# Gathering expert tokens by pairs of units, with one-hots as the stationary operand

## The chip, the cores and the metric

The kernel runs on one core of a Trainium2 chip. The metric is the time of one execution on the device in microseconds (us), as a median of several runs. Before the change the median of three runs was 1506.28 us (1504.05 to 1506.33).

## The reference

Two layers of one trunk. In each, a mixer (Fourier mixing, differential attention, a gated linear recurrence) is followed by a mixture of experts. Layer 0 computes 256 context and 256 latent tokens, layer 1 in the mixture only the latent ones. The part that matters here is the mixture; the reference sorts the token slots by expert, and for each block of one expert e does:

```python
D_MODEL = 1024; D_EXPERT = 512; N_EXPERTS = 32; TOP_K = 2
# wts: weight of a token's two experts; toks, ws: tokens and weights of a block's slots
xb = xpad[toks]
hb = jax.nn.silu(xb @ w1[e]) * (xb @ w3[e])
yb = (hb @ w2[e]) * ws[:, None]
acc = acc.at[toks].add(yb)
```

All weights are float32. One expert has six tiles of 1 MB, so the experts of both layers are 384 tiles, most of what the kernel reads.

## The kernel before

**Tiles.** S() gives a large tile of 128 x 2048 floats (1 MB) out of N_S = 22, W() a small one of 128 x 512 out of N_W = 11, PS() one of eight PSUM banks. Large tiles hold weights as they stream in, but also residuals, rows of modulation and split tokens. In the expert stage of layer 0, seven large tiles are taken otherwise: one of residuals, one of gating rows, four of tokens (hh and hl, the tokens' high and low parts) and the gathered tokens xt; a second xt lives for a while when the next group is gathered. In layer 1 it is four.

**The weight stream.** All weights form one list of tiles in the order of use. issue() (L169) writes their DMAs into the program of the SyncE (SP), which carries them out in order; a DMA waits until the tile that had its large tile before is released by its last reader. ahead(FIRST[l]) (L1711) asks for the first tiles of an expert stage, more() (L1612) for as many new ones as have been used up, ROOM[l] tiles ahead.

**Units.** The experts are ordered by how many tokens they have. units_of() (L31) makes units of 64 token slots: a unit serves one expert with 64 slots or two with 32 each. Two units are a pair (p), two pairs a group (g). Per pair moe() (L1365) does for each of two units: the ups (up, L1450: 64 slots times w1 and w3), act (L1461), transposing the hidden values (hid_t, L1466), and the downs (down, L1474: times w2). combine() (L1489) adds the pair before to the residuals while the ups of the next pair run. onehot_t() (L1436) makes the transposed one-hots for it.

**Before the first unit.** Routing ends with rmx (L1302), each token's place in each slot range. Then, in the order of the program: onehot(0) (L1385, one-hots of a group), order() (L1312, the experts' order, which the SyncE needs for addresses), late() (L1323, the routing weights, in three bfloat16 parts wb, and at its end the counts of an overflow), gather(0) (L1397), and the units. gather(g) has the tokens as the stationary operand and the one-hots moving, so that the result comes out transposed, as the ups want it; slot_weights() (L1417) casts the one-hots and multiplies them with wb. gather(g + 1) comes at the end of a group's second pair. No scheduler moves anything: each engine does its instructions in the order in which the program writes them, and waits for others by semaphores. PE is the TensorE, DVE the VectorE, ACT the ScalarE, POOL the GpSimd.

Of the kernel before, what the change touches and what calls it, by code (L numbers as in the profile page):

```python
# [50 lines left out]
NCOL = [3 * len(u) for u in UNITS]  # L51
N_S = 22
N_W = 11

# [15 lines left out]
def tile_backbone(  # L70
# [991 lines left out]
    def proj_prep(l, mixh, mixl, raw, pre, ends):  # L1062
# [242 lines left out]
        nw = nc_ // 6 * 4  # L1305
        wb = tiny([128, nt, nw, 3], "wb", 1, BF)
        wv = tiny([128, 2, nt], "wv", 1)
# [15 lines left out]
        def late():  # L1323
# [19 lines left out]

            for i in range(3):
                V.tensor_copy(wb[:, :, :, i], wx[0])
                if i < 2:
                    V.tensor_tensor(out=wx[0], in0=wx[0], in1=wb[:, :, :, i], op=OP.subtract)

# [12 lines left out]

        r.update(rmx=rmx, wb=wb, wv=wv, ec=ec, cap=cap, rem=rem, nbi=nbi, order=order, late=late)
        return r

    def moe(l, r):  # L1365
# [9 lines left out]

        def hsl(t, i, d):
            a = (i % 2) * D + d * 128
            return t[i // 2][:, a:a + 128]

        ohs, xts, wss, ots = {}, {}, {}, {}  # L1380

        def pairs_in(g):
            return min(2, np_ - 2 * g)

        def onehot(g):  # L1385

            o = tp.tile([128, 4, 2, 3, 64], FR, name="oh", tag="oh", bufs=1)
            n = pairs_in(g) * 6
            for i in range(nt):
                V.tensor_tensor(  # L1390
                    out=o[:, i].rearrange("p a b (h s) -> p (a b h) s", h=2)[:, 0:n],
                    in0=iota[:, None, :].to_broadcast([128, n, 32]),
                    in1=r["rmx"][:, i, 12 * g:12 * g + n][:, :, None].to_broadcast([128, n, 32]),
                    op=OP.is_equal)
            ohs[g] = o

        def gather(g):  # L1397

            o = ohs[g]
            m = pairs_in(g)  # L1400
            xt = S()
            for dd in range(4):
                ps = PS()
                for j in range(2):
                    d = 2 * dd + j
                    n = 0
                    for i in range(nt):
                        for t in (hh, hl):
                            mm(ps[:, j * 256:j * 256 + m * 128], hsl(t, i, d),
                               o[:, i, 0:m, 0:2].rearrange("p a b s -> p a (b s)"), n == 0, n == 2 * nt - 1)  # L1410
                            n += 1
                (V.tensor_copy if dd % 2 else A.copy)(v3(xt[:, dd * 512:(dd + 1) * 512], 256)[:, :, 0:m * 128],  # L1412
                                                      v3(ps, 256)[:, :, 0:m * 128])
            xts[g] = xt
            slot_weights(g)

        def slot_weights(g):  # L1417
            o = ohs[g]
            m = pairs_in(g)
            ob = wp.tile([128, 4, 256], BF, name="w", tag="w")  # L1420
            for i in range(nt):
                A.copy(ob[:, i, 0:m * 128].rearrange("p (a s) -> p a s", a=m),
                       f(o[:, i, 0:m, 0:2].rearrange("p a b s -> p a (b s)")))
            pw = PS()
            for pr in range(m):
                for i in range(nt):
                    mm(pw[:, pr * 16:pr * 16 + 12], ob[:, i, pr * 128:(pr + 1) * 128],
                       r["wb"][:, i, 4 * (2 * g + pr):4 * (2 * g + pr + 1), :].rearrange("p a b -> p (a b)"),
                       i == 0, i == nt - 1)
            ws = tiny([128, 2], "ws", 2)  # L1430
            for q in range(4):
                rr = slice(32 * q, 32 * q + 32)
                V.reduce_sum(ws[rr, 0:m], pw[rr, 0:16 * m].rearrange("p (a b) -> p a b", b=16)[:, :, 3 * q:3 * q + 3], axis=AX.X)
            wss[g] = ws

        def onehot_t(p):  # L1436

            o = ohs[p // 2]
            res = []
            for q in range(2):  # L1440
                pt = PS()
                for i in range(nt):
                    src = o[:, i, p % 2].rearrange("p b s -> p (b s)")[:, 64 * q:64 * q + 128]
# [181 lines left out]

        onehot(0)
        r["order"]()
        state["lim"] = first_1 + LIM if l == 0 else 1 << 30
        r["late"]()
        gather(0)  # L1630
        prev = None
        taken = {}
        for p in range(np_):
            sh = W()
            for q in range(2):
                u = 2 * p + q
                g = u // 4
# [5 lines left out]
                xt = xts[g]  # L1643
                m = u % 4
                end = u + 1 == len(units) and l in LAST
                if end:
                    px, py = PS(), PS()
                    down(ht, wd, px[0:64, :], py[64:128, :])
                ph = PS()
                for ks in UPS[q]:  # L1650
                    up(u, lambda k: xt[:, k * 256 + m * 64:k * 256 + (m + 1) * 64], ws, ph, ks)
# [3 lines left out]
                act(u, ph, wss[g][a:a + 64, m // 2:m // 2 + 1], sh)  # L1655
                if not again:
                    more(4 * len(ranks))
                if q == 0:
                    onehot_t(p)
                    if m == 2 and 4 * (g + 1) < len(units):  # L1660
                        onehot(g + 1)
                elif end:
                    spin(SPE[l], hh[0])
                else:
                    px, py = PS(), PS()
                    down(ht, wd, px[0:64, :], py[64:128, :])
                if q and units[u - 1][0] != ranks:
                    more(2 * len(wd))
                ht, wd = hid_t(u, sh, PS()), ws
            if p % 2 == 1 and u + 1 < len(units):  # L1670
                gather(g + 1)
            down(ht, wd, px[64:128, :], py[0:64, :])
# [127 lines left out]
```

## Time and profile before

| | |
|---|---|
| median of three runs | 1506.28 us |
| the profiled execution | 1505.11 us, of which 1503.3 us span from first to last instruction |
| busy: TensorE, VectorE, ScalarE, GpSimd | 1295.8, 623.1, 372.7, 364.8 us |
| moved by DMA | 489.66 MB, 326 GB/s over the span |
| expert stage of layer 0 | from about 339 us (routing done) to about 825 us |
| expert stage of layer 1 | from about 1037 us to the end |

The time of an engine that is busy tells little here: a stage has its own limit. The page's slices of the span show the DMA engines full in two long stretches and mostly not in the mixers, which lie before 310 and between 829 and 1030 us.

### The profile page before, as it was taken

Reading aid. Unit: us, or ns where it says so; the run is one execution under the profiler, and the core shown is the slowest. Engines: PE = TensorE matmul, PEld = TensorE weight load, DVE = VectorE, ACT = ScalarE, POOL = GpSimd, SP = SyncE. Lnnn points to the kernel's source line nnn. Section 1 sums busy time; section 2 is a strip of 40 time slices with the busy share of each in tenths; the row PEclk is TensorE's granted clock in tenths of the full one; section 3 lists DMA queues with packets and bytes.
Section 4 is the critical chain, followed back from the end, with each engine's and each line's share of the span. In section 5 each row is a group of like instructions: output and inputs, shape, how many; then the busy total and the mean of one; then the engine's idle time right before and its main releaser. Section 6 shows DMA issues by size and latency. Waiting matters only on the chain. (4 is left out here: it accounts for less than half of the span.)

```text
span 1503.3 us, 18776 instructions
## 1 busy us (share of the span) xinstructions
PE 1295.8 (86%) x6910; PEld 683.5 (45%) x6910; DVE 623.1 (41%) x1209; ACT 372.7 (25%) x763; POOL 364.8 (24%) x402
## 2 busy tenths in 40 slices
PE   5989998978999898989897999787989779787775
PEld 3767544765545353535352876365334223232231
DVE  3587587663333323232224678876212112111111
ACT  3333675321111110101012544842111001010010
POOL 2333012530243322222222551051111111101110
PEclk9999999988999999999999999898999999989898
DMA  9943352275999999999999924084999999999995
GB/s 346 388 151 120 119 207 93 85 305 204 421 421 405 421 420 421 420 421 421 420 421 386 383 91 136 34 312 186 420 420 420 421 421 420 421 421 421 421 421 244
DMA packets 101498, 489.66 MB, mean 326 GB/s; under 512 B 10411, under 2 KB 13081, under 8 KB 52249
## 3 DMA queue, kind: packets, MB, share of 16 engines
q1 hardware_dynamic: 96752, 485.11, 80.1%
q10 hardware_dynamic: 4649, 3.29, 0.8%
q8 instruction: 56, 0.92, 0.2%
q14 instruction: 41, 0.34, 0.1%
HBM read 487.32 MB, written 1.05 MB: 325 GB/s over the span
## 5 line engine op out<-in xcount | busy, mean ns | idle before, releaser
L125 PE MATMUL ps<-s 128*32 128x512 f32 (+3 forms) x2488 | 527.8, 611 | 85.0 <-DMA s<-in_w 81.1
L125 PEld LDWEIGHTS ps<-s 128*32 128x32 f32 (+2 forms) x2488 | 172.5, 138 | 398.3 <-issue 220.7
L1500 POOL TENSOR_TENSOR xres<-xres,w 128x512 f32<-128x512 f32 x92 | 116.7, 1295 | 420.6 <-DVE w L1499 420.6
L1464 DVE SCALAR_TENSOR_TENSOR w<-w,ws,ps 64x512 f32<-64x512 f32 x48 | 35.9, 747 | 402.2 <-ACT w L1463 402.2
L125 PE MATMUL ps<-s,ht 128*32 128x512 f32 (+1 forms) x1056 | 177.8, 596 | 8.0 <-ACT ht L1471 7.2
L125 PE MATMUL ps<-w,s 128*128 128x512 f32 x672 | 167.7, 402 | 1.3 <-POOL w L526 0.6
L1463 ACT ACTIVATE w<-ps 64x512 f32<-64x512 f32 x48 | 28.4, 592 | 553.5 <-PE ps L125 553.5
L1500 POOL TENSOR_TENSOR s<-s,w 128x512 f32<-128x512 f32 x50 | 63.2, 1287 | 364.6 <-DVE w L1499 364.6
L125 PEld LDWEIGHTS ps<-w,s 128*128 128x128 f32 x672 | 126.7, 192 | 33.5 <-issue 4.4
L526 POOL TENSOR_TENSOR w<-s,w 128x512 fp32r<-128x512 f32 x80 | 109.9, 1384 | 119.5 <-ACT w L525 101.1
L1499 DVE TENSOR_TENSOR w<-ps,s 128x512 f32<-128x512 f32 x148 | 91.1, 683 | 66.1 <-PE ps L125 66.1
L125 PE MATMUL ps<-s,w 128*128 128x512 f32 (+2 forms) x480 | 104.7, 369 | 5.2 <-DVE s L519 2.4
L125 PEld LDWEIGHTS ps<-s,ht 128*32 128x32 f32 (+1 forms) x1056 | 50.6, 122 | 111.4 <-issue 98.3
L125 PEld LDWEIGHTS ps<-s,w 128*128 128x128 f32 x480 | 78.0, 203 | 36.1 <-issue 13.9
L125 PE MATMUL ps<-w 128*128 128x512 f32 (+1 forms) x392 | 89.9, 381 | 2.4 <-ACT w L1485 1.4
L1486 DVE TENSOR_TENSOR w<-ps,w 128x512 fp32r<-128x512 f32 x48 | 30.9, 686 | 135.0 <-ACT w L1485 135.0
L125 PE MATMUL ps<-oh,s 128*128 128x256 f32 (+1 forms) x640 | 83.6, 293 | 0.0
L125 PEld LDWEIGHTS ps<-w 128*128 128x128 f32 x392 | 67.4, 198 | 34.6 <-issue 18.0
L125 PEld LDWEIGHTS ps<-oh,s 128*128 128x128 f32 x640 | 81.1, 202 | 3.2 <-issue 2.4
L1412 DVE COPY s<-ps 128x512 f32<-128x512 f32 (+1 forms) x26 | 16.8, 649 | 92.9 <-PE ps L125 86.2
L125 PE MATMUL ps<-s,cond 128*32 128x512 f32 x336 | 54.9, 637 | 0.0
L525 ACT CAST w<-s 128x512 fp32r<-128x512 f32 x80 | 48.3, 620 | 4.3 <-issue 1.4
(260 smaller groups left out, 1145.1 us busy)
## 6 DMA issues: line engine op xcount, KB each, us to landing
s<-in_w SPq DMA_DIRECT2D x384, 1024.0 KB, 19.8
s<-in_w_mod SPq DMA_DIRECT2D x48, 1024.0 KB, 12.5
s<-in_w_in SPq DMA_DIRECT2D x18, 1024.0 KB, 14.5
s<-in_w_out SPq DMA_DIRECT2D x8, 512.0 KB, 6.2
s<-in_w_out SPq DMA_DIRECT2D x4, 1024.0 KB, 8.7
s<-in_const_b SPq DMA_DIRECT2D x2, 768.0 KB, 15.4
s<-in_xc SPq DMA_DIRECT2D x2, 512.0 KB, 4.5
xres<-in_x SPq DMA_DIRECT2D x2, 512.0 KB, 7.5
```

The source lines that it names most:

```text
L125: PE.matmul(o, l, r, start=start, stop=stop)
L525: A.copy(wh[:, 0:n], src)
L526: G.tensor_sub(wl[:, 0:n], src, f(wh[:, 0:n]))
L1412: (V.tensor_copy if dd % 2 else A.copy)(v3(xt[:, dd * 512:(dd + 1) * 512], 256)[:, :, 0:m * 128], v3(ps, 256)[:, :, 0:m * 128])
L1463: A.activation(sh[a:a + 64, :], ps[a:a + 64, :], AF.Silu)
L1464: V.scalar_tensor_tensor(sh[a:a + 64, :], sh[a:a + 64, :], ws, ps[64 - a:128 - a, :], op0=OP.mult, op1=OP.mult)
L1486: V.tensor_sub(yl, ps, f(yh))
L1499: V.tensor_tensor(out=t, in0=ps, in1=g2[:, gg:gg + 512], op=OP.mult)
L1500: (V if end and h else G).tensor_add(xr_(tt, c), xr_(tt, c), t)
```

## The change

Tokens are gathered for one pair at a time. The one-hots are now the stationary operand and 512 columns of token rows move; the result has a slot per partition, is copied into two small tiles (rows), transposed (turn) and copied into two small tiles more (xts). The slot weights are multiplied with the one-hots as they are, wb has two float32r parts. A large tile less (N_S = 21), three small ones more (N_W = 14), and ROOM and FIRST of layer 0 are 15 instead of 14.

The order changes: gather(0) stands ahead of order(), turn(0) between order() and late(), the slot weights behind late(); the last part of late() becomes left(), called after the first unit. Later, gather(p + 1) stands ahead of the first downs of pair p, turn(p + 1) and slot_weights(p + 1) ahead of the second.

```diff
-N_S = 22
-N_W = 11
+N_S = 21
+N_W = 14
-        wb = tiny([128, nt, nw, 3], "wb", 1, BF)
+        wb = tiny([128, nt, nw, 2], "wb", 1, FR)
-            for i in range(3):
-                V.tensor_copy(wb[:, :, :, i], wx[0])
-                if i < 2:
-                    V.tensor_tensor(out=wx[0], in0=wx[0], in1=wb[:, :, :, i], op=OP.subtract)
+            V.tensor_copy(wb[:, :, :, 0], wx[0])
+            V.tensor_tensor(out=wb[:, :, :, 1], in0=wx[0], in1=f(wb[:, :, :, 0]), op=OP.subtract)
+
+        def left():
...
-        def onehot(g):
-            o = tp.tile([128, 4, 2, 3, 64], FR, name="oh", tag="oh", bufs=1)
+        def onehot(p):
+            o = tp.tile([128, 4, 3, 64], FR, name="oh", tag="oh", bufs=2)
...
-                            mm(ps[:, j * 256:j * 256 + m * 128], hsl(t, i, d),
-                               o[:, i, 0:m, 0:2].rearrange("p a b s -> p a (b s)"), n == 0, n == 2 * nt - 1)
+        def slots(p, i):
+            return ohs[p][:, i, 0:2].rearrange("p b s -> p (b s)")
+        def gather(p):
+            rows[p] = []
+            for h in range(2):
+                ps = PS()
+                n = 0
+                for i in range(nt):
+                    for t in (hh, hl):
+                        c = i % 2 * D + h * 512
+                        mm(ps, slots(p, i), t[i // 2][:, c:c + 512], n == 0, n == 2 * nt - 1)
+                        n += 1
+                t = W()
+                (V.tensor_copy if h else A.copy)(t, ps)
+                rows[p].append(t)
+        def turn(p):
+            xts[p] = []
+            for t in rows.pop(p):
+                ps = PS()
+                for k in range(4):
+                    PE.transpose(ps[:, k * 128:(k + 1) * 128], t[:, k * 128:(k + 1) * 128], ident)
+                x = W()
+                (V.tensor_copy if xts[p] else A.copy)(x, ps)
+                xts[p].append(x)
+        def slot_weights(p):
+            pw = PS()
             for i in range(nt):
-                A.copy(ob[:, i, 0:m * 128].rearrange("p (a s) -> p a s", a=m),
-                       f(o[:, i, 0:m, 0:2].rearrange("p a b s -> p a (b s)")))
+                mm(pw[:, 0:8], slots(p, i), r["wb"][:, i, 4 * p:4 * p + 4, :].rearrange("p a b -> p (a b)"),
+                   i == 0, i == nt - 1)
...
         onehot(0)
+        gather(0)
         r["order"]()
         state["lim"] = first_1 + LIM if l == 0 else 1 << 30
+        turn(0)
         r["late"]()
-        gather(0)
+        slot_weights(0)
...
-                    if m == 2 and 4 * (g + 1) < len(units):
-                        onehot(g + 1)
+                    if p + 1 < np_:
+                        onehot(p + 1)
+                    if p == 0:
+                        r["left"]()
...
                 else:
+                    if p + 1 < np_:
+                        gather(p + 1)
                     px, py = PS(), PS()
                     down(ht, wd, px[0:64, :], py[64:128, :])
...
-            if p % 2 == 1 and u + 1 < len(units):
-                gather(g + 1)
+            if p + 1 < np_:
+                turn(p + 1)
+                slot_weights(p + 1)
             down(ht, wd, px[64:128, :], py[0:64, :])
...
-    ROOM = 14, 17
-    FIRST = 14, 17
+    ROOM = 15, 17
+    FIRST = 15, 17
```

**Where instructions move.** First, the TensorE at the start of layer 0's expert stage, before. The row with utri is the last of routing, `ps<-w,ones 128x32` is order()'s matmul, `ps<-oh,s` the gather, `ps<-wb,w` the first of eight slot-weight matmuls, behind which stand the ups (`ps<-s 64x512`).

```order
L125 MATMUL ps<-w,utri 128x78
L125 LDWEIGHTS ones
L125 MATMUL ps<-w,ones 128x32
L125 MATMUL ps<-oh,s 128x256 x64
L125 LDWEIGHTS w
L125 MATMUL ps<-wb,w 128x12
```

And the same place now, to the first downs (`ps<-s,ht`). L1415 are the transposes of turn(), L1439 those of onehot_t(), L1464 those of hid_t().

```order
L125 MATMUL ps<-w,utri 128x78
L125 MATMUL ps<-s,oh 128x512 x16
L125 LDWEIGHTS ones
L125 MATMUL ps<-w,ones 128x32
L1415 MATMUL ps<-ca,w 128x128 x8
L125 MATMUL ps<-wb,oh 128x8 x4
L125 MATMUL ps<-s,w 64x512 x16
L1439 MATMUL ps<-ca,oh 128x128 x8
L1464 MATMUL ps<-ca,w 128x64 x4
L125 MATMUL ps<-s,w 64x512 x16
L125 MATMUL ps<-s,oh 128x512 x16
L125 MATMUL ps<-s,ht 64x512 x8
```

The gather has moved ahead of order()'s matmul; transposes and slot weights stand between that matmul and the ups; and the gather of pair 1 stands between the second unit's ups and the first downs.

Second, the VectorE at the same place, before. L1390 are the one-hots, L1315 to L1321 order(), from L1325 on late().

```order
L1302 TENSOR_TENSOR rmx<-w 128x312
L1390 TENSOR_TENSOR oh<-ca,rmx 128x384 x4
L1315 SCALAR_TENSOR_TENSOR w<-w,ca 128x32
L1316 TENSOR_REDUCE w<-w 128x1
L1318 TENSOR_TENSOR w<-ca,w 128x32
L1321 TENSOR_SCALAR idx<-ps 1x32
L1325 TENSOR_TENSOR w<-w 128x16
```

And now; L1406 is the copy of the gather's second half, L1417 the copy of its transpose.

```order
L1302 TENSOR_TENSOR rmx<-w 128x312
L1382 TENSOR_TENSOR oh<-ca,rmx 128x192 x4
L1406 COPY w<-ps 128x512
L1315 SCALAR_TENSOR_TENSOR w<-w,ca 128x32
L1316 TENSOR_REDUCE w<-w 128x1
L1318 TENSOR_TENSOR w<-ca,w 128x32
L1321 TENSOR_SCALAR idx<-ps 1x32
L1417 COPY w<-ps 128x512
L1325 TENSOR_TENSOR w<-w 128x16
```

Two copies out of PSUM have come in between, one ahead of order() and one ahead of late().

## Rows read from the trace of the kernel before

**Rows 1.** Stretches: PE, PEld, DVE, ACT, POOL busy; PEclk, DMA share, GB/s.

```profile
339.00:356.00 17.00, 14.61 (x93) 11.98 (x95) 9.72 (x38) 4.20 (x10) 0.00 (x0) 0.77 0.00 1
356.00:812.00 456.00, 421.45 (x2410) 195.79 (x2407) 137.47 (x225) 60.01 (x127) 122.16 (x97) 0.98 1.01 417
1032.00:1050.00 18.00, 11.28 (x62) 7.87 (x64) 12.50 (x46) 3.46 (x8) 0.00 (x0) 0.81 0.01 1
1050.00:1483.00 433.00, 358.68 (x1920) 124.45 (x1917) 71.49 (x132) 42.34 (x94) 49.71 (x40) 0.93 1.01 420
```

**Rows 2.** Timeline of the issuing queue after the gaps: start, length, what.

```profile
355.65 0.80 SPq L177 DMA_DIRECT2D s<-in_w  x2
1049.04 0.94 SPq L177 DMA_DIRECT2D s<-in_w  x2
```

**Rows 3.** Chain of waits, end of layer 0 and layer 1: start, length, what.

```profile
814.58 14.87 DMA s<-in_w_in
...
1149.58 19.75 DMA s<-in_w
```

**Rows 4.** Timeline, start of layer 0's expert stage: start, length, engine, line, operands, count.

```profile
338.83 1.97 DVE L1390 TENSOR_TENSOR oh<-ca,rmx 128x384 fp32r<-128x384 f32 x4
340.71 0.18 DVE L1315 SCALAR_TENSOR_TENSOR w<-w,ca 128x32 f32<-128x32 f32 x1
...
341.39 0.21 PE L125 MATMUL ps<-w,ones 128*128 128x32 bf16 x1 [3.70 <-DVE w L1318]
...
341.44 10.33 PE L125 MATMUL ps<-oh,s 128*128 128x256 f32 x64
...
341.75 0.15 DVE L1325 TENSOR_TENSOR w<-w 128x16 f32<-128x16 f32 x1
...
344.68 0.38 DVE L1347 TENSOR_TENSOR w<-w,wb 128x208 f32<-128x208 f32 x1
...
351.62 0.42 PE L125 MATMUL ps<-wb,w 128*128 128x12 bf16 x8
...
351.97 7.09 PE L125 MATMUL ps<-s 128*64 128x512 f32 x32
```

**Rows 5.** Timeline, start of layer 1's expert stage.

```profile
1037.21 1.03 DVE L1390 TENSOR_TENSOR oh<-ca,rmx 128x384 fp32r<-128x384 f32 x2
...
1038.87 6.00 PE L125 MATMUL ps<-oh,s 128*128 128x256 f32 x32
...
1039.17 0.14 DVE L1325 TENSOR_TENSOR w<-w 128x8 f32<-128x8 f32 x1
...
1041.53 0.25 DVE L1347 TENSOR_TENSOR w<-w,wb 128x88 f32<-128x88 f32 x1
...
1044.41 1.27 DVE L1412 COPY s<-ps 128x512 f32<-128x512 f32 x2
...
1045.37 7.09 PE L125 MATMUL ps<-s 128*64 128x512 f32 x32
```

**Rows 6.** TensorE at half clock (a stretch) and at full clock (timeline).

```profile
341.40:346.90 5.50, 5.50 (x26) 0.50 0.01 3
...
358.99 1.09 PE L1444 MATMUL ps<-ca,oh 128*128 128x128 f32 x8
...
379.85 3.94 PE L125 MATMUL ps<-w 128*128 128x512 f32 x16
```

**Rows 7.** TensorE in two stretches late in layer 0: busy, clock, DMA.

```profile
790.00:794.00 4.00, 1.42 (x8) 1.00 1.01 420
794.00:797.50 3.50, 3.50 (x20) 0.51 1.02 421
```

**Rows 8.** A stretch just behind layer 0's restart; columns as in rows 1.

```profile
362.00:372.00 10.00, 10.00 (x49) 3.39 (x46) 0.74 (x1) 0.59 (x1) 0.00 (x0) 1.00 0.98 388
```

**Rows 9.** Waits in layer 1's mixer: us in total, times, longest.

```profile
ACT w L547 <- PE ps L125: 5.5, 6, 1.4
...
PE ps L125 <- DVE w L379: 3.8, 2, 2.5
```

More of the change, by code (lines that the diff above doesn't have):

```diff
@@ L1360, in late @@
             V.tensor_copy(nbi, nbs)
-        r.update(rmx=rmx, wb=wb, wv=wv, ec=ec, cap=cap, rem=rem, nbi=nbi, order=order, late=late)
+        r.update(rmx=rmx, wb=wb, wv=wv, ec=ec, cap=cap, rem=rem, nbi=nbi, order=order, late=late, left=left)
         return r
@@ L1374, in odd @@
             return ap.rearrange("p (j m i) -> p j m i", m=128, i=2)[:, k // 2, :, k % 2]
-        def hsl(t, i, d):
-            a = (i % 2) * D + d * 128
-            return t[i // 2][:, a:a + 128]
         ohs, xts, wss, ots = {}, {}, {}, {}
-        def pairs_in(g):
-            return min(2, np_ - 2 * g)
-        def onehot(g):
-            o = tp.tile([128, 4, 2, 3, 64], FR, name="oh", tag="oh", bufs=1)
-            n = pairs_in(g) * 6
+        def onehot(p):
+            o = tp.tile([128, 4, 3, 64], FR, name="oh", tag="oh", bufs=2)
@@ L1389, in onehot @@
             for i in range(nt):
                 V.tensor_tensor(
-                    out=o[:, i].rearrange("p a b (h s) -> p (a b h) s", h=2)[:, 0:n],
-                    in0=iota[:, None, :].to_broadcast([128, n, 32]),
-                    in1=r["rmx"][:, i, 12 * g:12 * g + n][:, :, None].to_broadcast([128, n, 32]),
+                    out=o[:, i].rearrange("p b (h s) -> p (b h) s", h=2),
+                    in0=iota[:, None, :].to_broadcast([128, 6, 32]),
+                    in1=r["rmx"][:, i, 6 * p:6 * p + 6][:, :, None].to_broadcast([128, 6, 32]),
@@ L1394, in onehot @@
                     op=OP.is_equal)
[L1395 to L1402, printed above, removed]
-                ps = PS()
[L1404 to L1408, printed above, removed]
-                            mm(ps[:, j * 256:j * 256 + m * 128], hsl(t, i, d),
-                               o[:, i, 0:m, 0:2].rearrange("p a b s -> p a (b s)"), n == 0, n == 2 * nt - 1)
[L1411 to L1420, printed above, removed]
-            for i in range(nt):
-                A.copy(ob[:, i, 0:m * 128].rearrange("p (a s) -> p a s", a=m),
-                       f(o[:, i, 0:m, 0:2].rearrange("p a b s -> p a (b s)")))
[L1424 to L1430, printed above, removed]
+            ohs[p] = o
@@ new lines, in slots @@
+        def slots(p, i):
+            return ohs[p][:, i, 0:2].rearrange("p b s -> p (b s)")
+        rows = {}
+        def gather(p):
+            rows[p] = []
+            for h in range(2):
+                ps = PS()
+                n = 0
[7 more added lines that the diff above has]
+                rows[p].append(t)
@@ new lines, in turn @@
+        def turn(p):
[9 more added lines that the diff above has]
+            pw = PS()
+            for i in range(nt):
+                mm(pw[:, 0:8], slots(p, i), r["wb"][:, i, 4 * p:4 * p + 4, :].rearrange("p a b -> p (a b)"),
+                   i == 0, i == nt - 1)
+            ws = tiny([128, 1], "ws", 2)
@@ L1431, in slot_weights @@
             for q in range(4):
                 rr = slice(32 * q, 32 * q + 32)
-                V.reduce_sum(ws[rr, 0:m], pw[rr, 0:16 * m].rearrange("p (a b) -> p a b", b=16)[:, :, 3 * q:3 * q + 3], axis=AX.X)
-            wss[g] = ws
+                V.reduce_sum(ws[rr], pw[rr, 2 * q:2 * q + 2], axis=AX.X)
+            wss[p] = ws
         def onehot_t(p):
-            o = ohs[p // 2]
+            o = ohs[p]
             res = []
@@ L1442, in onehot_t @@
                 for i in range(nt):
-                    src = o[:, i, p % 2].rearrange("p b s -> p (b s)")[:, 64 * q:64 * q + 128]
+                    src = o[:, i].rearrange("p b s -> p (b s)")[:, 64 * q:64 * q + 128]
                     PE.transpose(pt[:, i * 128:(i + 1) * 128], f(src), ident)
@@ L1636, in moe @@
                 u = 2 * p + q
-                g = u // 4
                 ranks, base = units[u]
@@ L1642, in moe @@
                 ws = taken[ranks]
-                xt = xts[g]
-                m = u % 4
                 end = u + 1 == len(units) and l in LAST
@@ L1650, in moe @@
                 for ks in UPS[q]:
-                    up(u, lambda k: xt[:, k * 256 + m * 64:k * 256 + (m + 1) * 64], ws, ph, ks)
+                    up(u, lambda k: xts[p][k // 4][:, k % 4 * 128 + q * 64:k % 4 * 128 + (q + 1) * 64], ws, ph, ks)
                     if q == 0 and prev is not None and ks[0] == 0:
@@ L1654, in moe @@
                 a = 64 * q
-                act(u, ph, wss[g][a:a + 64, m // 2:m // 2 + 1], sh)
+                act(u, ph, wss[p][a:a + 64], sh)
                 if not again:
```

## The prediction

> **What bounds the kernel now.** I read the transfers first. In the view by stretches the DMA engines are busy all the time from 356 to 812 us and from 1050 to 1483 us, at 417 and 420 GB/s, and idle from 339 to 356 and from 1032 to 1050 [rows 1]. Those two idle stretches are the starts of the expert stages: every slot is full and the queue can go on only when the TensorE has used up a weight tile. The view of the DMA-issuing queue shows it: after the gap the first weight tile is asked for at 355.65 us in layer 0 and at 1049.04 in layer 1 [rows 2]. The chain of waits says the same from its end. Layer 0 hands over to layer 1 by a transfer that starts at 814.58 and lands at 829.45; in layer 1 the chain is one transfer of 19.8 us after another [rows 3]. So each expert stage takes its bytes at a fixed rate, and the end of the kernel moves one to one with the two restarts. TensorE work behind a restart costs nothing as long as the queue stays filled; in front of it every microsecond counts.
>
> What stands in front of a restart is read in the timeline [rows 4, 5]. In layer 0: one-hots from 338.83, order() on the VectorE from 340.71 and its matmul at 341.39, the gather from 341.44 to 351.77, slot weights at 351.62, and the ups of the first unit from 351.97. The queue restarts 3.7 us later, when half of the 32 records of the ups (7.09 us) are through. late() runs on the VectorE from 341.75, inside the gather's time, and is hidden by it.
>
> **The change part by part.**
>
> *Gather of one pair.* 64 matmuls of 256 columns go, 16 of 512 come (8 in layer 1). At half clock 26 records of 256 columns took 5.5 us, 0.21 each [rows 6], so 0.42 for 512; at full clock 16 of 512 took 3.94 us, 0.25 each [rows 6]. The one-hot operations are half as long, and the gather now stands in front of order(), so the TensorE need not wait for 341.39: four operations took 1.97 us [rows 4], one of half the columns is put at 0.3, and the gather starts at 339.1. Layer 0: 16 matmuls take 6.7 us at half clock and 3.9 at full; before, the clock rose at 346.9 after 5.5 us of work [rows 6], and work now starts 2.3 us earlier, so I let it rise at 344.5. The gather ends at 345.2 (bounds 343.0 and 346.0), 6.6 us earlier than before. Layer 1: one-hots start at 1037.21 [rows 5], the gather at 1037.5, eight matmuls at half clock end at 1040.9 (at full clock 1039.5), where they ended at 1044.87.
>
> *The new serial chain.* The rows of order in the section on the change show what follows on the VectorE: the copy of the second half, order(), the copy of the second transpose, and only then late(). On the TensorE order()'s matmul stands ahead of the transposes, and the slot weights, which need late()'s result, stand ahead of the ups. So what the gather hid is now in a row: copy 0.65 (two took 1.27, rows 5), order() up to its matmul 0.68 (340.71 to 341.39), the matmul 0.21, eight transposes 1.09 (row of 8, rows 6), copy 0.65, late() from its first operation to the first subtraction's end 3.31 (341.75 to 345.06), and four slot-weight matmuls 0.3 (eight took 0.42) [rows 4]. Sum 6.9 us: the ups start at 352.1, with handovers between engines at 352.4, against 351.97, so +0.4 us. With the bounds of the gather, and with transposes that take twice as long at half clock, -2.1 to +2.0. Behind the waiting slot weights on the TensorE stand the ups, and for them waits the DMA queue. Layer 1 has a shorter gather to gain from: late() takes 2.61 (1039.17 to 1041.78, rows 5), the chain 6.1, and 7.2 with the transposes at half clock; the ups start at 1047.9 with handovers, against 1045.37: +2.5 us (0.2 to 2.8).
>
> *The clock at the ups.* Before, ten or six microseconds of gather without a hole stood ahead of the ups, which ran at full clock. Now the TensorE has about 1.5 us of work between the gather's end and the ups. The nearest rows: in 790 to 794 us it was busy 1.42 of 4 us, and in the next 3.5 us the granted clock was 0.51 although it worked throughout [rows 7]. So the ups most likely begin at half clock. The first half of them takes 3.5 us at full clock and 7.1 at half: between 0 and +3.5 us for each layer; I take about half, +1.8 and +1.7, since in layer 0 the clock came back after 5.5 us of work [rows 6]. The Trainium skill ("TensorE: Matmul & The Clock Gate", section "HAM oscillation — how this bites in real kernels") tells of kernels that start each burst cold because the burst before is shorter than the wait behind it. By that rule alone both first halves would be cold throughout, and the sum below would come to 1515.8 us; the rows show a return within 5.5 us, so I stay with half.
>
> *The slot.* Before, at the restart of layer 0, 22 slots less one residual, one row tile, four tiles of tokens and one gathered tile leave 15 for weights; now 21 less six leave 15. In layer 1 it is 18 both times (22 less 4, 21 less 3). The second gathered tile lived only later. So no weight tile more is loaded when the gap begins, the gap ends at the same release, and one more tile ahead is worth nothing; if it were loaded, one megabyte at 420 GB/s is 2.5 us, in layer 0 alone.
>
> *Pairs behind the restart.* The gather of pair 1 now comes in the first pair. Per pair that is 3.9 + 1.1 + 0.3 us, as much as half of the old group's 10.33. It is hidden as long as the queue is filled; in layer 0 it is thinly filled just behind the restart (362 to 372 us: 388 GB/s instead of 420 [rows 8]). Bounds 0 and +5.3; I take +0.4, as the ups of two units have freed eight tiles by then. The eight ScalarE casts per group that go, and left(), which now runs beside the ups, cost and give nothing: neither engine is in front of a transfer there.
>
> *Small tiles, 14 for 11.* In layer 1's mixer (829 to 1032 us) the ScalarE waits for matmuls to release small tiles, 5.5 us in six waits at one line, and the TensorE itself waits 3.8 us for the modulation rows of line 379 [rows 9]. A ScalarE that waits for a release by a TensorE at work costs nothing. Bounds -3.8 and 0; I take -0.8, near zero, because the line-379 waits end with VectorE work that stays.
>
> **Sum.** Layer 0 +0.4 +1.8 = +2.2; layer 1 +2.5 +1.7 = +4.2; mixer -0.8; pairs +0.4: together +6.0 us. The profiled execution took 1505.1 us (span 1503.3), the median of the runs is 1.2 higher, 1506.3. So 1511.1 on the profiled scale and 1512 us as a median.
>
> **Rivals.** A: the clock holds through the holes. Then +0.4 +2.5 -0.8 +0.4 = +2.5, 1508.8 us, no change that can be measured (this kernel's runs can tell about 0.2%, 3 us). For it: in layer 0 the clock came back after 5.5 us of work [rows 6], and the new gather is as long; against it rows 7. B: the shorter gather reaches the ups, because slot weights or late() do not hold them. Then the ups start right behind the second copy: 345.2 + 0.65 + 1.09 + 0.65 + 0.3 = 347.9, -4.1 us, in layer 1 1043.5, -1.9, with the mixer -6.4 in all: 1500 us, faster. It decides if late() stands ahead of the copies on the VectorE; the rows of order say it doesn't. C: the small tiles are worth all that the two rows of waits in the mixer show, -9.3 instead of -0.8: 1503.8 us. For it: the number of such waits; against: the TensorE works while it is waited for. D: the queue runs dry behind layer 0's restart, because gather, transposes and slot weights of pair 1 come before any of the second pair's ups: +5.3 instead of +0.4, 1517 us. For it rows 8; against it the 20 us of transfers that eight released tiles make.
>
> **Chances.** Forecast 0.45, A 0.2, B 0.1, C 0.15, D 0.1. The forecast's own range is 1508 to 1516. For 8 in 10 the range goes from 1501.5, which takes in C and leaves out most of B, to 1517.5. Faster by over 0.2% (below 1503.3): B, half of C and a little of the rest, 0.2. Within 0.2%: most of A, the other half of C and the forecast's low tail, 0.3. Slower: 0.5.
>
> **What would show it.** In the new profile, the ups of the first unit starting near 352.4 and, counted from the one-hots' start, 10.7 us behind it in layer 1; the slot weights waiting for the VectorE; the granted clock at half when these ups begin; the first issue behind the gaps some 2 and 4 us later, counted from the one-hots; transfers at 420 GB/s without a hole from there on. I am wrong if the ups begin before 350, if the clock stays at full, or if the two full stretches of transfers have holes or have become shorter.

## The result, and the profile after

The changed kernel takes 1520.59 us (median of 5 runs, 1518.87 to 1525.92), the kernel before 1505.87: a ratio of 1.0112, interval 1.0101 to 1.0123. It is slower by 1.1%, 14.7 us. The forecast was 1512 with a range up to 1517.5: the sign was right, the size was not. The profiled execution of the changed kernel is the longest of its five (1525.92 us, span 1523.8), so its trace differs from that of before by 20.5 us; the sums below are made on the two traces.

The view by stretches of the changed kernel, with the columns of [rows 1]:

```profile
344.20:365.00 20.80, 14.85 (x51) 8.36 (x53) 6.48 (x27) 2.97 (x6) 0.00 (x0) 0.72 0.11 43
365.00:815.00 450.00, 426.95 (x2252) 193.05 (x2250) 157.29 (x286) 58.48 (x112) 120.47 (x96) 0.97 1.00 412
...
1043.00:1072.00 29.00, 17.20 (x60) 8.91 (x60) 13.29 (x51) 2.96 (x6) 0.00 (x0) 0.65 0.18 66
1072.00:1505.00 433.00, 367.63 (x1918) 129.74 (x1915) 84.27 (x180) 45.86 (x94) 49.69 (x40) 0.93 1.01 420
```

Layer 1's transfers run as before. Layer 0's are at 412 GB/s and no longer 417. The issuing queue, to be read beside [rows 2] and, in its middle row, [rows 3]:

```profile
363.95 0.80 SPq L177 DMA_DIRECT2D s<-in_w  x2
...
828.83 2.50 SPq L177 DMA_DIRECT2D s<-in_w_in  x1
...
1070.13 4.35 SPq L177 DMA_DIRECT2D s<-in_w  x4
```

With the first one-hots of each layer (338.83 and 1037.21 before [rows 4, 5], 344.20 and 1052.48 after) and the starts of the ups, these marks cut both executions into pieces. The mark in_w_in is the third issue of layer 1's projection weights; in every run the first of them comes 5.2 to 5.5 us earlier.

| piece | before | after | change | forecast |
|---|---|---|---|---|
| start to layer 0's one-hots | 338.83 | 344.20 | +5.37 | 0 |
| one-hots to ups | 13.14 | 13.86 | +0.72 | +0.4 |
| ups to first issue | 3.68 | 5.90 | +2.22 | +1.8 |
| first issue to in_w_in (layer 0's stage) | 458.93 | 464.88 | +5.95 | +0.4 |
| in_w_in to layer 1's one-hots (mixer) | 222.63 | 223.65 | +1.02 | -0.8 |
| one-hots to ups | 8.15 | 11.38 | +3.23 | +2.5 |
| ups to first issue | 3.68 | 6.27 | +2.59 | +1.7 |
| first issue to the end | 454.28 | 453.63 | -0.65 | 0 |

The chain in front of layer 0's ups, the timeline of the changed kernel (compare [rows 4]):

```profile
344.20 1.16 DVE L1382 TENSOR_TENSOR oh<-ca,rmx 128x192 fp32r<-128x192 f32 x4
...
344.70 5.88 PE L125 MATMUL ps<-s,oh 128*128 128x512 f32 x16 [1.58 <-DVE oh L1382]
...
350.62 0.69 DVE L1406 COPY w<-ps 128x512 f32<-128x512 f32 x1 [5.26 <-PE ps L125]
...
351.98 0.19 PE L125 MATMUL ps<-w,ones 128*128 128x32 bf16 x1 [1.40 <-DVE w L1318]
...
352.02 1.07 PE L1415 MATMUL ps<-ca,w 128*128 128x128 f32 x8
...
353.20 0.69 DVE L1417 COPY w<-ps 128x512 f32<-128x512 f32 x1 [0.81 <-PE ps L1415]
353.80 0.17 DVE L1325 TENSOR_TENSOR w<-w 128x16 f32<-128x16 f32 x1
...
356.62 0.38 DVE L1345 TENSOR_TENSOR wb<-w,wb 128x208 fp32r<-128x208 f32 x1
...
357.14 0.98 PE L125 MATMUL ps<-wb,oh 128*128 128x8 f32 x4 [4.05 <-DVE wb L1345]
...
358.06 8.45 PE L125 MATMUL ps<-s,w 128*64 128x512 f32 x28
```

Each link is where the forecast put it: copy, order(), its matmul, transposes, copy, late(), slot weights, ups. The idle time in brackets shows the two waits for the VectorE, 1.40 and 4.05 us. By stretches, the TensorE ahead of the ups and in their first half, in layer 0 and in layer 1:

```profile
349.00:355.70 6.70, 2.69 (x16) 1.81 (x14) 3.51 (x16) 2.38 (x6) 0.00 (x0) 1.00 0.00 0
355.75:362.50 6.75, 5.36 (x16) 2.29 (x18) 1.77 (x8) 0.08 (x1) 0.00 (x0) 0.50 0.00 0
1048.70:1069.00 20.30, 11.75 (x34) 6.25 (x36) 8.47 (x33) 2.96 (x6) 0.00 (x0) 0.50 0.00 1
```

In layer 0 the granted clock fell to the lower of its two levels (1.2 GHz) behind 6.7 us with 2.69 us of work. In layer 1 it was there from before the one-hots until most of the first half of the ups was through; the TensorE's rows there, with [rows 5] to compare:

```profile
1052.89 3.78 PE L125 MATMUL ps<-s,oh 128*128 128x512 f32 x8 [1.11 <-DVE oh L1382]
...
1058.05 1.95 PE L1415 MATMUL ps<-ca,w 128*128 128x128 f32 x8
...
1063.37 0.56 PE L125 MATMUL ps<-wb,oh 128*128 128x8 f32 x2 [3.38 <-DVE wb L1345]
...
1063.86 9.68 PE L125 MATMUL ps<-s,w 128*64 128x512 f32 x32
```

The Trainium skill ("TensorE: Matmul & The Clock Gate", section "HAM oscillation — how this bites in real kernels") says that a burst shorter than the wait behind it leaves the next one to start cold. In layer 0 the trace agrees: 1.07 us of transposes stand ahead of the wait of 4.05 us, and the ups start at 0.50; in layer 1 the clock was already at 0.50 before the gather. The price, 2.22 and 2.59 us, lies between the forecast's half and the 3.5 us that it gave for that rule alone.

What the forecast did not have, apart from the first row of the table, is in layer 0's stage. The same view, cut at the holes in the transfers:

```profile
365.00:400.00 35.00, 34.52 (x168) 16.26 (x164) 13.02 (x31) 4.72 (x9) 5.38 (x5) 1.00 1.00 408
400.00:402.00 2.00, 1.54 (x12) 0.86 (x8) 0.76 (x2) 1.14 (x2) 2.00 (x2) 1.00 0.77 225
402.00:453.00 51.00, 50.53 (x292) 24.20 (x294) 18.70 (x33) 7.26 (x14) 12.73 (x11) 1.00 1.00 409
453.00:456.00 3.00, 3.00 (x18) 1.00 (x16) 0.40 (x3) 0.00 (x0) 0.00 (x0) 1.00 0.38 79
456.00:466.00 10.00, 10.00 (x48) 4.84 (x46) 6.16 (x10) 1.07 (x2) 4.97 (x5) 1.00 0.97 398
466.00:468.00 2.00, 1.95 (x14) 0.90 (x10) 0.38 (x1) 1.00 (x2) 2.00 (x3) 1.00 0.32 78
468.00:815.00 347.00, 325.41 (x1716) 144.99 (x1718) 117.86 (x209) 43.28 (x84) 93.40 (x75) 0.96 1.01 419
```

From the restart to 468 us the TensorE is never without work for long (34.52 of 35 us, 50.53 of 51), and the transfers have three holes (DMA share 0.77, 0.38, 0.32). The kernel before, in the same part of its stage:

```profile
365.00:453.00 88.00, 85.85 (x484) 40.17 (x480) 29.57 (x48) 12.73 (x26) 27.31 (x22) 1.00 1.00 415
453.00:468.00 15.00, 14.71 (x112) 7.03 (x113) 5.20 (x7) 1.98 (x5) 3.13 (x3) 1.00 0.97 395
```

There too the TensorE is busy nearly throughout (85.85 of 88 us) while the DMA engines are just kept full. It has next to no time there in which it could make up for added work. What stands in the TensorE's first pair, from its timeline:

```profile
376.50 4.00 PE L125 MATMUL ps<-s,oh 128*128 128x512 f32 x16
380.43 3.65 PE L125 MATMUL ps<-s,ht 128*64 128x512 f32 x16
384.01 0.69 PE L1464 MATMUL ps<-ca,w 64*128 64x64 f32 x4
384.63 1.09 PE L1415 MATMUL ps<-ca,w 128*128 128x128 f32 x8
385.48 0.59 PE L125 MATMUL ps<-wb,oh 128*128 128x8 f32 x4
386.00 3.65 PE L125 MATMUL ps<-s,ht 128*64 128x512 f32 x16
```

The gather of pair 1 (4.00 us), its transposes and slot weights stand among the downs of pair 0, which free weight tiles. Two releases show the effect: first both in the kernel before, then the same two tiles of the stream in the changed one.

```profile
370.03 0.33 SPq L177 DMA_DIRECT2D s<-in_w  x1
...
439.22 0.33 SPq L177 DMA_DIRECT2D s<-in_w  x1
```

```profile
382.40 0.33 SPq L177 DMA_DIRECT2D s<-in_w  x1
...
454.38 0.33 SPq L177 DMA_DIRECT2D s<-in_w  x1
```

Counted from the first issue the first one moves from 14.38 to 18.45 us, and the second, behind the gather of pair 3, from 83.57 to 90.43: 4.1 and 6.9 us late. By then the changed kernel has done the gathers, transposes and slot weights of pairs 1, 2 and 3 (4.00 + 1.09 + 0.59 = 5.7 us each). The kernel before gathers pairs 0 and 1 ahead of its restart and the next two only at the end of pair 1, in one piece:

```profile
400.70 7.94 PE L125 MATMUL ps<-oh,s 128*128 128x256 f32 x64
```

### The profile page after: what moved, and what is told of

Same layout as the page of the kernel before. It is cut to its first block, busy times and chain, and to the rows that moved or that the text cites. A ratio compares the mean times of both kernels' runs of the same rounds, so it can differ in the third digit from the quotient of the medians.

```text
span 1523.8 us, 18635 instructions
## 1 busy us (share of the span) xinstructions
PE 1326.0 (87%) x6758; PEld 688.1 (45%) x6758; DVE 658.2 (43%) x1303; ACT 373.0 (24%) x745; POOL 368.2 (24%) x402
## 5 line engine op out<-in xcount | busy, mean ns | idle before, releaser
L125 PE MATMUL ps<-s,w 128*32 128x512 f32 (+4 forms) x2592 | 542.5, 602 | 75.6 <-DMA s<-in_w 67.6
L125 PEld LDWEIGHTS ps<-s,w 128*32 128x32 f32 (+2 forms) x2592 | 190.6, 144 | 396.6 <-issue 238.9
L526 POOL TENSOR_TENSOR w<-s,w 128x512 fp32r<-128x512 f32 x80 | 114.2, 1438 | 122.4 <-ACT w L525 93.8
L125 PE MATMUL ps<-s 128*128 128x512 f32 (+3 forms) x376 | 94.3, 445 | 1.2 <-ACT s L705 1.2
L125 PE MATMUL ps<-s,oh 128*128 128x512 f32 x296 | 79.0, 417 | 2.7 <-DVE oh L1382 2.7
L125 PEld LDWEIGHTS ps<-s 128*128 128x128 f32 (+1 forms) x376 | 61.2, 193 | 26.5 <-issue 6.1
L125 PEld LDWEIGHTS ps<-s,oh 128*128 128x128 f32 x296 | 56.2, 197 | 33.2 <-issue 19.9
L1417 DVE COPY w<-ps 128x512 f32<-128x512 f32 x24 | 16.6, 692 | 102.8 <-PE ps L1415 102.8
L1466 ACT COPY ht<-ps 128x256 f32<-128x256 f32 x48 | 17.9, 373 | 146.1 <-PE ps L1464 146.1
```

Source lines behind the costliest of these rows:

```text
L125: PE.matmul(o, l, r, start=start, stop=stop)
L526: G.tensor_sub(wl[:, 0:n], src, f(wh[:, 0:n]))
L1417: (V.tensor_copy if xts[p] else A.copy)(x, ps)
L1466: A.copy(ht, pt[:, 0:256])
```

## The experiments

The pieces of the table above, in the profile of each kernel (us). In the last column of ups_first_s22, best1, best2 and best3 the first issue is that of a further tile, which has a slot of its own; the first issue that waits for a release comes 5.27 us behind the ups in best2 and 3.68 in the other three.

| kernel | layer 0's one-hots | to ups | to first issue | stage | mixer 1 | to ups | to first issue |
|---|---|---|---|---|---|---|---|
| late_gather | 342.56 | 13.86 | 5.90 | 466.40 | 222.35 | 11.38 | 6.16 |
| spins | 341.91 | 13.38 | 3.68 | 465.25 | 222.75 | 10.54 | 3.68 |
| ups_first | 342.31 | 9.12 | 3.68 | 465.95 | 222.98 | 7.45 | 4.69 |
| before_w14 | 340.19 | 13.09 | 3.68 | 461.09 | 222.54 | 8.57 | 3.68 |
| no_g12 | 342.02 | 13.83 | 5.88 | 458.46 | 223.25 | 11.38 | 6.25 |
| no_g89 | 342.82 | 13.91 | 5.92 | 465.38 | 223.21 | 11.38 | 6.25 |
| early1 | 341.60 | 13.39 | 3.68 | 461.23 | 223.30 | 11.12 | 3.68 |
| ups_first_s22 | 341.04 | 9.79 | 3.68 | 463.22 | 222.22 | 6.70 | -0.42 |
| w11 | 342.65 | 14.02 | 6.07 | 465.43 | 223.53 | 11.46 | 6.11 |
| before_again | 339.66 | 12.49 | 3.68 | 458.57 | 222.24 | 8.12 | 3.68 |
| best1 | 343.42 | 9.62 | 3.68 | 463.57 | 222.35 | 7.61 | 0.86 |
| best2 | 340.98 | 9.92 | 3.68 | 457.44 | 227.87 | 7.15 | 0.86 |
| after_order | 341.99 | 13.87 | 5.90 | 459.19 | 222.71 | 11.39 | 6.17 |
| before_order | 339.69 | 12.54 | 3.68 | 457.93 | 222.85 | 8.15 | 3.68 |
| best3 | 340.28 | 9.90 | 3.68 | 457.41 | 222.07 | 7.81 | 0.86 |

**late_gather.**

```diff
-                    if p + 1 < np_:
-                        gather(p + 1)
                     px, py = PS(), PS()
...
             if p + 1 < np_:
+                gather(p + 1)
                 turn(p + 1)
```

> The changed kernel, with the gather of the next pair taken from ahead of the pair's first downs and put directly ahead of its transposes, behind the hidden rows' transposes of the pair's second unit. Theory: layer 0's queue runs dry because that gather (3.9 us) delays the release of weight tiles in the first pairs; then the holes in the transfers (400-402, 453-456, 466-468 us in the changed kernel's profile) shrink to the one of before, first issue behind the gap to the first transfer of the next layer's projection weights takes about 459 us (before 458.93, changed 464.88), and the time falls by about 6, to 1514.6 us. Rival: the gather's time is on the path wherever it stands in the first pairs, the holes only move: 464 to 465 us for that stretch and 1520 +- 1.5 us.

1522.77 us, 1.0121 of before (1.0106 to 1.0137). The rival holds: the stage is 466.40, even a little above its 464 to 465. My first theory, that the gather's place within a pair matters, falls; what is left of it is that its work comes in these pairs at all.

**spins.**

```diff
         gather(0)
+        spin(3, hh[0])
         r["order"]()
...
         r["late"]()
+        spin(8, hh[0])
```

> The changed kernel with 3 idle matmuls of 512 columns behind the first gather and 8 behind the transposes, in the TensorE's waits for the VectorE; nothing else is moved. Theory (the clock): the first unit's ups run at full clock, the first issue comes 3.7 us behind their start and no longer 5.9 (layer 0) and 6.3 (layer 1): -2.2 and -2.6, so about 1515.8 us. Rival (the chain alone): the clock stays at half for the ups, the idle matmuls last until the slot weights could start or longer, and the time is unchanged or up to 2 us more: 1520 to 1523 us.

1516.58 us, 1.0088 (1.0074 to 1.0102). The theory holds: 3.68 us from the ups to the first issue in both layers. The ups also start earlier, 13.38 and 10.54 us behind the one-hots (13.86 and 11.38). The stretch of layer 0's ups in its profile, where the changed kernel's had 0.50:

```profile
355.30:362.00 6.70, 6.70 (x33) 2.20 (x32) 0.62 (x4) 0.00 (x0) 0.00 (x0) 1.00 0.28 88
```

**ups_first.**

```diff
         r["late"]()
-        slot_weights(0)
...
                 a = 64 * q
+                if u == 0:
+                    slot_weights(0)
                 act(u, ph, wss[p][a:a + 64], sh)
```

> The changed kernel with the slot weights of pair 0 moved behind the ups of the first unit, so that the ups no longer stand behind late(). Theory (the serial chain): the ups start about 0.3 us behind the second copy of the transposed tokens, 9.7 us behind the one-hots' start in layer 0 (changed 13.9, before 13.1) and 8.5 in layer 1 (changed 11.4, before 8.2); the first issue moves by -4.1 and -2.9 if the clock at the ups is as it was, and the time is about 1513.6 us. Rival (the clock): the ups start that much earlier, but they run at half clock for longer, the first issue moves by under 1.5 us in each layer: 1517.5 to 1520 us.

1512.41 us, 1.0050 (1.0036 to 1.0064). The serial chain behind late() cost 4.74 us in layer 0 and 3.93 in layer 1, and without that wait the clock held in layer 0 (3.68); in layer 1 the ups began at half clock (4.69; mean granted clock of their first half 0.78). Layer 0's first issue now comes 12.80 us behind the one-hots, 4 us sooner than before the change, and yet the kernel is slower than before: the stage is still 465.95, and layer 0's one-hots come 3.5 us later.

**before_w14.**

```diff
-N_S = 22
-N_W = 11
+N_S = 21
+N_W = 14
...
-    ROOM = 14, 17
-    FIRST = 14, 17
+    ROOM = 13, 16
+    FIRST = 13, 16
```

> The kernel before with 14 small tiles and 21 slots (and one weight tile less ahead: 13 and 16), its gather unchanged. Read in the profile: the start of the first one-hots in layer 0 (before 338.83 us, changed 344.20), and the mixer of layer 1 from the first transfer of its projection weights to the one-hots (before 222.6 us, changed 223.7). Theory: one slot less makes the mixer of layer 0 slower, the one-hots start at 342 to 344 us; the small tiles give nothing in layer 1. Rival: the mixer does not depend on them and the one-hots' 5.4 us were of that execution, 338 to 340 us here. The one tile less ahead costs 2.5 us at each restart: about 1511 us by the rival, 1514.5 by the theory.

1512.15 us, 1.0050 (1.0036 to 1.0064). Layer 1's mixer does not see the small tiles (222.54). One weight tile less ahead lengthens layer 0's stage by 2.2 us and what follows layer 1's first issue by 3.8, from 454.28 to 458.12: the price of a tile that the forecast named, 2.5 us, is of the right size in layer 0 and low in layer 1. The one-hots come at 340.19, just above the rival's 338 to 340 and below the theory's 342 to 344.

**no_g12 and no_g89.** The calls for two pairs of layer 0 are left out:

```diff
-                    if p + 1 < np_:
+                    if p + 1 < np_ and not (l == 0 and p + 1 in (1, 2)):
                         gather(p + 1)
...
-            if p + 1 < np_:
+            if l == 0 and p + 1 in (1, 2):
+                xts[p + 1], wss[p + 1] = xts[p], wss[p]
+            elif p + 1 < np_:
                 turn(p + 1)
                 slot_weights(p + 1)
```

> The changed kernel without the gather, transposes and slot weights of pairs 1 and 2 of layer 0 (these pairs reuse the tokens and slot weights of pair 0, so part of the computation is left out). Read: the stretch from the first issue behind layer 0's gap to the hand-over transfer of layer 1's projection weights (before 458.93 us, changed 464.88). Theory: layer 0's first pairs are bound by the TensorE's work, and some 10.6 us less of it there closes the holes: 459 to 460 us. Rival: the holes come from the slots (one fewer, and held otherwise), not from that work: 464 to 466 us.

> The same edit for pairs 8 and 9 of layer 0 instead of 1 and 2 (part of the computation is left out). Theory: once the queue has filled, the transfers bound the stage and the same work costs nothing: the stretch stays at 464 to 466 us. Rival: all of layer 0's stage is bound by the TensorE: 459 to 460 us.

1516.62 and 1524.03 us, one execution each. This separates the theories: without pairs 1 and 2 the stage is 458.46, without pairs 8 and 9 it is 465.38. The release that came 90.43 us behind the first issue in the changed kernel, and 83.57 in the one before, comes at 80.88 in no_g12. Where the changed kernel had its second and third holes, the profile of no_g12 has none:

```profile
451.00:454.00 3.00, 3.00 (x15) 1.07 (x15) 2.37 (x4) 0.00 (x0) 3.00 (x3) 1.00 1.01 418
464.00:466.00 2.00, 2.00 (x11) 1.42 (x8) 0.75 (x1) 0.60 (x1) 0.00 (x0) 1.00 1.01 422
```

**early1.**

```diff
         onehot(0)
+        onehot(1)
         gather(0)
...
         r["late"]()
+        gather(1)
         slot_weights(0)
```

(In the loop, one-hots and gather of the next pair begin with pair 1.)

> The changed kernel with the one-hots of pair 1 made before the first gather and the gather of pair 1 put between the transposes of pair 0 and its slot weights, in both layers, where the TensorE waits for late(). Theory: it takes the place of the idle matmuls of the run with spins, keeps the clock up for the ups (first issue 17.1 us behind the one-hots in layer 0, 14.2 to 14.6 in layer 1), and takes 4 us of TensorE work out of pair 0: layer 0's stretch falls from 465.3 to 461 us, the time is about 1512.5 us. Rival: the gather only moves from behind the restart to in front of it, where it counts one to one, and the first issue comes 2 to 4 us later than with spins: 1516.5 to 1519 us.

1513.23 us, 1.0051 (1.0038 to 1.0063), near the theory's 1512.5 and under the rival's range. Without pair 1's gather behind the restart the stage is 4.0 us shorter than with spins (461.23 and 465.25), and the release at 90.43 us comes at 86.38. So here the work counts one to one. Its TensorE timeline, where 3.98 us of gather fill the wait for late():

```profile
349.43 1.07 PE L1415 MATMUL ps<-ca,w 128*128 128x128 f32 x8
350.25 3.98 PE L125 MATMUL ps<-s,oh 128*128 128x512 f32 x16
354.45 0.61 PE L125 MATMUL ps<-wb,oh 128*128 128x8 f32 x4 [0.22 <-DVE wb L1345]
354.99 1.51 PE L125 MATMUL ps<-s,w 128*64 128x512 f32 x6
```

**ups_first_s22.** N_S 22, N_W 12, ROOM and FIRST 16 and 18, one buffer of one-hots, on ups_first.

> The kernel of the run ups_first with one slot more (22), paid for by 12 small tiles instead of 14 and by one buffer of one-hots instead of two, and with 16 and 18 weight tiles ahead instead of 15 and 17. Theory: one tile more is really loaded before each gap, the queue's gaps end with one megabyte more done: -2.5 us in each layer, 1507.4 us on that run's scale (1512.4). Rival: the queue ahead is not what bounds, or the fewer small tiles cost as much: 1511 to 1513 us.

1505.54 us, 0.9999 (0.9990 to 1.0007): 6.9 less than ups_first, where the theory had 5. In layer 0 the stage is 2.7 shorter, in layer 1 the first issue (there the further tile itself) comes 6.28 us behind the one-hots and not 12.14. The mixers changed as well (1.3 us earlier one-hots in layer 0, 0.8 less in mixer 1), so not all of the 6.9 is the slot.

**w11 and before_again.** The changed kernel with N_W = 11, and the kernel before once more.

> The changed kernel with 11 small tiles, as before, and all else as changed. Theory: the small tiles give nothing and cost nothing: the mixer of layer 1 (first projection transfer to the one-hots) stays at 222.3 to 223.7 us, the first one-hots of layer 0 start at 341 to 344 us as in the changed kernel's other executions, the time is 1520 +- 2 us. Rival: with 14 small tiles the TensorE's waits in layer 0's mixer fall so that the clock drops two times more; with 11 the one-hots start at 338.8 to 340 us and the time is 1517 us. A third way: the gathered rows and tokens need the three tiles, the expert stages become slower, 1523 us or more.

> The kernel before, unchanged, for a second profile of layer 0's mixer. Theory: its six stretches at half clock ahead of the first one-hots belong to the kernel, the one-hots start at 338.3 to 339.5 us again. Rival: they belong to that execution, and the one-hots start anywhere up to 344 us.

1522.79 us, 1.0113 (1.0097 to 1.0128), which is the changed kernel's own ratio (1.0112), and 1503.80 in one execution. The three small tiles are worth nothing, in either mixer or stage. The kernel before repeats its layer 0 mixer: the one-hots come at 339.66, just above the theory's 339.5. One part of what the changed kernel loses in that mixer is seen at a wait of the TensorE near 190 us. In the kernel before, in before_again and in ups_first_s22 (22 slots):

```profile
190.10 0.44 PE L866 MATMUL ps<-ca,w 128*128 128x128 f32 x2 [0.52 <-DVE w L860]
```

```profile
189.64 0.44 PE L866 MATMUL ps<-ca,w 128*128 128x128 f32 x2 [0.80 <-DVE w L860]
```

```profile
189.99 0.44 PE L866 MATMUL ps<-ca,w 128*128 128x128 f32 x2 [1.00 <-DVE w L860]
```

and in w11 (21 slots), with the stretch behind it:

```profile
190.86 0.69 PE L866 MATMUL ps<-ca,w 128*128 128x128 f32 x2 [1.71 <-DVE w L860]
```

```profile
190.90:194.20 3.30, 3.30 (x9) 2.77 (x10) 3.27 (x6) 3.00 (x8) 0.00 (x0) 0.50 0.00 0
```

With 21 slots the wait comes in one piece, and in the profiles of the changed kernel and its eight variants with 21 slots the clock is at half behind it, by estimate 1.7 us of loss (half of 3.3 to 3.4 us); in those with 22 it is not. before_w14 has the same wait of 1.71 us and no fall, so the wait alone does not decide it. Nor is the slot most of that mixer's loss: the four variants with 22 slots reach the one-hots at 340.28 to 343.42 us, the kernel before at 338.83 and 339.66.

**best1, best2.** On ups_first_s22: order() behind turn(0); then also layer 0's units with the second unit of two experts directly behind the first. BETWEEN counts the single experts ahead of each unit of two.

```diff
         gather(0)
+        turn(0)
         r["order"]()
         state["lim"] = first_1 + LIM if l == 0 else 1 << 30
-        turn(0)
```

```diff
-BETWEEN = (3, 2, 2, 3, 2, 3, 3), ...
+BETWEEN = (3, 0, 2, 2, 3, 2, 3, 3), ...
```

> The kernel of the run ups_first_s22 with order() behind the transposes of pair 0 instead of ahead of them. Theory: the ups start 0.7 us earlier behind the one-hots in both layers (9.1 and 6.0 us; 9.79 and 6.70 in that run), and the time falls by 1 to 1.4 us against that run, to about 1504 us, the same as before. Rival: the clock, at half for longer, takes it back: 1505 to 1506 us.

> The kernel of best1 with layer 0's units in another order: the second unit of two experts directly behind the first, and the expert of two units behind it, as layer 1 has it. Theory: layer 0's first pairs are bound by the TensorE's work; a unit of two experts brings twelve weight tiles of transfers for one unit's work and the second unit of one expert brings none, so the queue does not run dry: the stretch from the first issue to layer 1's projection weights falls from 463 to 459 us, and the time to about 1500 us, 0.3% under the kernel before. Rival: the holes only move to later pairs, or the single experts at the stage's end hold up the hand-over: 1504 us or more.

1505.34 us, 1.0001 (0.9992 to 1.0010), and 1506.33, 1.0008 (0.9999 to 1.0017). best1 misses: its time is the rival's, but not for the rival's reason. The ups come 9.62 and 7.61 us behind the one-hots, because order()'s matmul, which waits for the VectorE, now stands between the transposes and the ups; and layer 1's further tile, whose expert order() names, is asked for later (0.86 behind the ups, not 0.42 ahead). In best2 the stage is 457.44, but the mixer is 5.5 us longer, as the rival on the single experts at the stage's end expected; the cause of those 5.5 us is tested only by the next order, which ends as before and does not have them.

**after_order, before_order, best3.** An order that ends as before does, on the changed kernel, on the kernel before and on best1:

```diff
-BETWEEN = (3, 2, 2, 3, 2, 3, 3), ...
+BETWEEN = (3, 0, 2, 3, 4, 3, 3), ...
```

> The changed kernel with layer 0's units in another order at the start alone: the second unit of two experts directly behind the first; the stage ends with three single experts and a unit of two, as it did. Theory (the queue runs dry at the start): first issue to layer 1's projection weights 459 to 460 us (changed 464.88), from there to layer 1's one-hots 222 to 224 us as before, one execution at about 1516 us. Rival (the TensorE's whole work in layer 0): the first falls and the second rises by as much, their sum stays at 688 to 689 us (changed 688.53), 1521 us.

> The kernel before with the same order of layer 0's units. Theory: its queue hardly runs dry (one hole of 0.7 us at 452), so the sum of the two stretches stays within 1.5 us of 681.6, 1502.5 to 1505 us. Rival: the order itself is better for any kernel: the sum falls by 3 us or more.

> The kernel of best1 with that order of layer 0's units. Theory: stage 459 to 460 us (best1 463.57), mixer 222.4, time 1501 us, 0.25% under the kernel before. Rival: as in best2 the mixer takes it back, 1505 to 1506 us.

after_order takes 1516.73 us and before_order 1504.85, one execution each; best3 takes 1498.52, 0.9961 of before (0.9948 to 0.9975). The theory holds in all three; best3's stage, 457.41, is even under its 459 to 460. Stage and mixer together are 681.90 us in after_order (688.53 in the changed kernel, the same work in another order), 680.78 in before_order (681.56 before) and 679.48 in best3. So the loss was an empty queue at the stage's start and not the TensorE's whole work. Layer 1, whose units stand in such an order in both kernels, fits: it loses nothing behind its restart (-0.65), though its gathers are half as long. best3 is faster than both kernels: against before its trace gains 3.2 us at each restart, 1.5 in the stage and 0.6 in mixer 1, and loses 1.4 in layer 0's mixer.

## Why the prediction was wrong

- **The step that failed** is "Pairs behind the restart", +0.4 us: layer 0's stage measured +5.95. Its ground, that the ups of two units have freed eight tiles by then, is true and too short. Eight issues do fall into the first 13.2 us, and they carry the transfers over the gather of pair 1: the first hole comes only at 400 us. But the TensorE has next to no idle time in this part of the stage, in the kernel before too (85.85 of 88 us), so what is put into it is not made up. The releases are 4.1 us late behind the gather of pair 1 and 6.9 behind that of pair 3, and the queue runs dry three times before 468 us. Shown by no_g12, no_g89, early1 and after_order: the release at 90.43 us comes at 86.38 in early1 and 80.88 in no_g12, and the stage falls from 465 to 461.23 and 458.46.
- **Rival D** was this, at 5.3 us; I gave it 0.1. That its size is so near is in part luck, as it counted pair 1 alone and three pairs are at work. The forecast also set 5.3 us per pair against half of the old group's 10.33 us, which ran largely at half clock; behind the restart the same 64 matmuls take 7.94. The view by stretches of before [rows 1] shows the mean of the whole stage, and [rows 8] its thin start, which I saw and priced too low. Of the prediction's own signs of being wrong, holes in the transfers came true.
- **Gather**: forecast to end 6.4 us behind the one-hots in layer 0, measured 6.38; in layer 1 3.7, measured 4.2.
- **Serial chain**: right, +0.72 and +3.23 for +0.4 and +2.5. Too small were the slot weights, 0.98 us at half clock for 0.3; with the clock held up (spins) the chain is +0.24 and +2.39. In layer 1 the forecast's 1047.9 is neither of its two cases (1047.0 and 1048.1 before handovers) but lies between them.
- **Clock at the ups**: right in kind, +2.22 and +2.59 for +1.8 and +1.7, shown by spins. Rival A, that it holds, is out.
- **Slot**: right that no further tile is loaded ahead of the gap (15 and 18 in both kernels), and that one would be worth about 2.5 us (2.2 and 3.8 in before_w14, 2.7 in layer 0 of ups_first_s22).
- **Small tiles**: worth nothing (w11), so not even -0.8, and rival C is out. The mixer's +1.02 is no more than executions differ: with the same mixer late_gather has 222.35. Rival B's chain is what ups_first makes of layer 0 (ups 9.12 us behind the one-hots for 9.1; layer 1 7.45 for 6.3); it needed late() off the path, as the prediction said.
- **Not in the sum** at all, and the second step that failed: layer 0's mixer, put at nothing without a reason. It measured +5.37 in this trace, 2 to 4 us in the variants with 21 slots and 0.6 to 4.6 in those with 22, against the two traces of before. By estimate 1.7 us of it, with 21 slots alone, is the clock behind the wait near 190 us. The rest differs from execution to execution; its cause stays open.

The sum of the terms was 6.0 and came out as 20.5 us on the trace, 14.7 as a median.

## What to carry to other kernels

A stage whose transfers look full on average may be bound by its consumer at its start. Cut the view by stretches there: where the consumer is busy nearly throughout and the transfers are only just full, count every microsecond that a change puts into the consumer as if it stood in front of the restart, and add it up over all the units until the queue has filled, not over the first one. That the issuing queue waits for releases says little by itself: it does so in both kernels. When parallel work is cut into a shorter but serial chain, fill its waits with work that would come later anyway (early1), or move what nobody needs yet off it (ups_first); in layer 0 both also kept the clock. And put units that bring many bytes for little work early in such a stage.

## What the runs showed of the hardware

Behind a wait of the TensorE of 1.40 us and one of 4.05 with 1.07 us of work between them, the granted clock was 0.50 for the next 6.8 us, while in layer 0 idle matmuls in the same waits kept it at 1.00 (spins). In layer 1 a gather of 3.78 us without a pause, at half clock, did not bring the clock back, and it stayed at 0.50 for 20 us in all. Four slot-weight matmuls of 8 columns, with 128 columns of one-hots stationary, took 0.98 us at half clock and 0.59 at full, where eight of 12 columns, in bfloat16 with casts of the one-hots, took 0.42 before [rows 4].
